# A two-layer decoder step on one core: one unit of output weights, the product's last right sides and its buffers moved in program order

## The chip, the cores and the metric

The kernel runs on one core of a Trainium2 chip. The metric is the device time of one execution in microseconds, lower is better. A launch does one step of the whole trunk: weights and inputs come from HBM, and every output goes back there.

## The reference, cut to what matters

Two layers over a stream of 1,024 prompt tokens, 64 sample tokens and 16 meta tokens (1,104 columns of 1,024 features; the second layer has no meta columns and works on 1,088). The first layer is a Mamba-2 mixer, the second sliding-window attention over shared keys and values; each is followed by an MLP with a squared ReLU:

```python
def sq_relu_mlp(h, norm_w, w_up, w_down):
    return h + jnp.square(jax.nn.relu(rmsnorm(h, norm_w) @ w_up)) @ w_down

# second layer
hp = hp + swa_prompt(q_p, k_p, v_p, k_meta, v_meta, attn_sinks[j]) @ w_o[j]
hp = sq_relu_mlp(hp, mlp_norm_w[layer], w_up[layer], w_down[layer])
```

`w_o` is 1,024 x 1,024, `w_up` 1,024 x 4,096. The change touches the product with `w_o` in the second layer and the product with `w_up` in both.

## The kernel before, in words

**Precision.** Every product of float32 numbers is made of three matmuls: each operand is split into a high part, rounded to a shorter format by a cast on ScalarE, and a low part, the rest, by a subtraction on VectorE (activations) or GpSimd (weights). `mm3` (L199 to L206) issues the three, at L204 (high by high), L205 (high weight by low activation) and L206 (low weight by high activation). So a weight's high part is needed first, its low part two matmuls later.

**Weights.** `wunit` (L156) brings one unit of weights. In the first layer it loads the raw weight into a tile `raw` (2 buffers), casts it on ScalarE (L170) and subtracts on GpSimd (L171). In the second layer most units were split before and lie in HBM as a pair, so two loads by SyncE's queue (L163) bring both parts. The tiles `w` are a ring of 6, which is 3 units.

**Order.** The program is written in one order, and a planner, run when the kernel is built, gives every engine its own fixed order from it by an estimate of when each operand is ready; a place in a buffer is given out in program order, and an operation in a new tile waits for the last reader of what lay there. Each engine, and each DMA queue, then works strictly in its order.

**Second layer, attention's end.** `attention` (L1588 on) works through the heads and chunks of columns, and returns the last four of its output units: chunk 1, the second half of the heads, v = 0 to 3. `out_unit` (L1654) loads its weights and makes two blocks of 128 output rows, 24 matmuls in all, then adds the residual, splits the result and hands it to the stream. Before these four, `second_layer` closes attention's pool `ap`, makes X, a tile of the stream (8 x 1,088 per partition), and `stream.load` (L124, its loads at L128) reads the two finished chunks of the stream back from HBM into X and normalises them there; chunk 1 comes from the four units directly.

**The up product.** The first four of 32 column blocks of `w_up` are computed plainly (`plain_up`, L1015; two at a time in the second layer, three and one in the first). The other 28 go in 14 pairs (`up`, L1117; `up_pair`, L1070) by a Strassen-Winograd scheme on 2 x 2 blocks: seven products of sums instead of eight. Left sides are sums of weight blocks (`up_weights`, L1051): a11, s1 = a21 + a22 (the first sum, L1057), a11 - a21 (L1057), s1 - a11 (L1063), a12, a22, a12 - s1. `raw2` loads the pair's raw weights; every third raw tile lies in the pool `rx`, with the sums `s` (2 buffers) and the results `rx`. `wparts` splits a left side: cast on ScalarE (L1047), subtraction on GpSimd (L1048).

**The right sides.** `sides` (L985) makes the seven right sides from the normalised activations, once for both halves k = 0, 1 of the columns. `step(i, k)` forms one of them and splits it (cast at L1011, subtraction at L1012, here called its split):

- 0: b11; 4: b21; 6: b22, as they are;
- 1: t = b12 - b11; 2: b12 = b22 - b12; 3: t = b22 - t; 5: t = b21 - t (subtractions at L989).

In the first layer the activations lie in `hh`, t is b11's own place, and steps 0, 4 and 6 aren't run: those parts lie in S, split for the plain product already. In the second layer they lie in X, t is one of two temporaries (pool `ts`, on the right side of the memory), and steps 0, 4, 5 and 6 write into S, over the columns that the plain product has read; steps 1 to 3 write tiles `T`. The k = 1 half of step 4 writes columns of chunk 1, the last chunk that the plain product reads. Pools are stacks on a left and a right side. After the steps the second layer closes `ts` and the pool of X, places R0 (the buffer for the down product's right side) where X was, and calls `up`, whose pool `rx` comes on the left, above R0.

**Chain.** The pair's first tile is a11 by step 0 (bank `ma`), the second s1 by step 1 (`md` in the first pair), the third a11 - a21 by step 2 (`mc`), the fourth s1 - a11 by step 3 (`mb`); 24 matmuls each for k = 0 and 1 together. Steps 4, 5 and 6 are used by the fifth to seventh. R0 gets its first blocks by SyncE's queue (L1140) during the pairs, and they are split at L1145 and L1146; R0 is multiplied after the up product.

Of the kernel before, what the change touches and what calls it, by code (L numbers as in the profile page):

```python
# [9 lines left out]
F32R = mybir.dt.float32r  # L10
# [6 lines left out]
P = 128  # L17
# [6 lines left out]
META = SEQ + NB * NS  # L24
NM = 16
T = META + NM
# [115 lines left out]
class Kernel:  # L142
# [842 lines left out]
    def sides(self, X, qw, tiles, temps=None):  # L985


        nc = self.nc
        tt = lambda out, x, y: nc.vector.tensor_tensor(out=out, in0=x, in1=y, op=ALU.subtract)  # L989
        at = lambda j, q: tuple(self.S[:, e, 4 * j:4 * j + 4, q * qw:q * qw + qw] for e in range(2))  # L990
        self.qw = qw
        self.xo = [{0: at(0, q), 4: at(1, q), 5: at(0, p), 6: at(1, p)} for q, p in PAIRS]
        B = [[[X[:, 4 * j:4 * j + 4, q * qw:q * qw + qw] for q in qs] for j in range(2)] for qs in PAIRS]

        def step(i, k):
            (b11, b12), (b21, b22) = B[k]
            t = b11 if temps is None else temps[k]
            src = {0: b11, 1: t, 2: b12, 3: t, 4: b21, 5: t, 6: b22}[i]
            if i == 1:
                tt(t, b12, b11)  # L1000
            elif i == 2:
                tt(b12, b22, b12)
            elif i == 3:
                tt(t, b22, t)
            elif i == 5:
                tt(t, b21, t)
            if i not in self.xo[k]:
                o = tiles()
                self.xo[k][i] = o[:, 0], o[:, 1]
            hi, lo = self.xo[k][i]  # L1010
            nc.scalar.copy(out=hi, in_=src)  # L1011
            nc.vector.tensor_tensor(out=lo, in0=src, in1=hi.bitcast(F32), op=ALU.subtract)  # L1012
        return step

    def plain_up(self, layer, fs, chs, rd, rs=None):  # L1015

# [50 lines left out]
        yield self.wparts(a22, sh)  # L1067
        yield self.wparts(add(a12, s1, ALU.subtract), sh)

    def up_pair(self, layer, f, rd, rt):  # L1070


        nc = self.nc
        qw = self.qw
        n = 2 * qw
        banks = {}
        tt = lambda out, x, y: nc.vector.tensor_tensor(out=out, in0=x, in1=y, op=ALU.add)
        tmp = lambda: self.n3().rearrange("p a b -> p (a b)")[:, :n]
        r = self.rx.tile([P, 4, n], F32, tag="rx", bufs=1, name="rx")

        for i, (wh, wl) in enumerate(self.up_weights(layer, f)):
            b = self.CHAIN[f % 2][i]
            first = b not in banks
            if first:
                banks[b] = self.pq.tile([P, 1024], F32, tag=b, bufs=1, name="m" + b)
            for k in range(2):
                xh, xl = self.xo[k][i]
                self.mm3(banks[b][:, 512 + (k - 1) * qw:512 + k * qw], [(wh[:, q], wl[:, q]) for q in range(4)],
                         [(xh[:, q], xl[:, q]) for q in range(4)], first)
            pv = banks[b][:, 512 - qw:512 + qw]  # L1090
            if i == 0:
                m1 = tmp()
                nc.scalar.copy(out=m1, in_=pv)
            elif i == 1:
                nc.scalar.copy(out=r[:, 3], in_=pv)
            elif i == 2:
                tt(r[:, 3], pv, r[:, 3])
            elif i == 3:
                u = tmp()
                tt(u, pv, m1)  # L1100
                tt(r[:, 3], r[:, 3], u)
            elif i == 4:
                nc.scalar.activation(out=r[:, 0], in_=pv, func=AF.Relu)
            else:
                tt(r[:, 7 - i], pv, u)
            e = {3: 3, 4: 0, 5: 2, 6: 1}.get(i)
            if e is None:
                continue
            if i != 4:
                nc.scalar.activation(out=r[:, e], in_=r[:, e], func=AF.Relu)  # L1110
            nc.scalar.activation(out=r[:, e], in_=r[:, e], func=AF.Square)
        if not 2 <= f < 14:
            nc.sync.dma_start(out=rd[f].rearrange("p f (i n) -> p (f i) n", i=2), in_=r)
            return
        self.side_sums([r[:, e] for e in range(4)], rt[(f - 2) // KB][:, :, :, (f - 2) % KB], m1, u)

    def up(self, layer, rd, rt, R0):  # L1117

        with ExitStack() as cq:
            self.rx = self.pool("rx", ctx=cq)  # L1120
            self.ws = self.rx
            self.rawi = 0
            self.pq = self.pool("pq", space=PSUM, ctx=cq)
            for f in range(2, 16):
                self.up_pair(layer, f, rd, rt)
                if f == 8:
                    self.block_load(rd, 0, R0)
                if f > 11:
                    self.block_parts(f - 12, R0)

    def load_stream(self, big, h_d):

# [518 lines left out]
                half, sp = 0, None  # L1651
        return outs

    def out_unit(self, c, n, prs, v, a, xs, stream):  # L1654

        nc = self.nc
        ws = [self.wunit(self.i["w_o"][pr, v], 4, 256, key=("o", pr, v)) for pr in prs]
        last = prs[-1] == 1
        for m in range(2):
            u, ms = 2 * v + m, slice(m * P, m * P + P)  # L1660
            pt = self.gps()[:, :n]
            self.mm3(pt, [(wh[:, k, ms], wl[:, k, ms]) for wh, wl in ws for k in range(4)],
                     [tuple(e[:, :n] for e in x) for x in a])
            xh, xl = (x[:, u, :n] for x in xs[c])
            h = stream.place(c, u, n) if last else self.n1("hs")[:, :n]
            nc.vector.tensor_tensor(out=h, in0=pt, in1=xl.bitcast(F32), op=ALU.add)
            nc.vector.tensor_tensor(out=h, in0=h, in1=xh.bitcast(F32), op=ALU.add)
            nc.scalar.copy(out=xh, in_=h)
            (nc.vector if c == 1 and last else nc.gpsimd).tensor_tensor(out=xl, in0=h, in1=xh.bitcast(F32),
                                                                        op=ALU.subtract)  # L1670
            if last:
                stream.done(c, u, h)
# [110 lines left out]
    def first_layer(self, cb):  # L1783
# [6 lines left out]
        with ExitStack() as ch:  # L1790
# [20 lines left out]
                self.out_last(hts, done, norm)  # L1811
            with ExitStack() as ct:
                tp = self.pool("T", ctx=ct)
                step = self.sides(big, T // 4, lambda: tp.tile([P, 2, 4, T // 4], F32R, tag="T", bufs=6, name="T"))
                with ExitStack() as ce:
                    self.banks(ce, 8)
                    plain = self.plain_up(0, (0, 1, 2), dict(enumerate(CH)), rd)
                    next(plain)
                    norm(2)
                    for _ in plain:  # L1820
                        pass
                    for _ in self.plain_up(0, (3,), dict(enumerate(CH)), rd):
                        pass
                for i in (1, 2, 3, 5):
                    for k in range(2):
                        step(i, k)
                ch.close()
                R0 = self.pool("R0", ctx=ch, right=True).tile([P, 2, 4, T], F32R, name="R0")
                self.up(0, rd, rt, R0)
# [12 lines left out]
    def second_layer(self, nx, cb):  # L1842
# [6 lines left out]
        with ExitStack() as cx:  # L1849
            cr = ExitStack()  # L1850
            with ExitStack() as c1:
# [11 lines left out]
                tmp = self.pool("att", ctx=cr, right=True)  # L1863
                stream = Stream(self, chs, h_d, self.ncol(3), ps)
                outs = self.attention(nx, ap, tmp, ps, chs, stream)
            stream.load(self.pool("X", ctx=cx).tile([P, KT, META], F32, name="X"))
            for e in outs:
                self.out_unit(*e)
            cr.close()
            tp = self.pool("T", ctx=cr, right=True)  # L1870
            with ExitStack() as ce:
                ts = self.pool("ts", ctx=ce, right=True)
                temps = [ts.tile([P, 4, qw], F32, name="t%d" % k) for k in range(2)]
                step = self.sides(stream.X, qw, lambda: tp.tile([P, 2, 4, qw], F32R, tag="T", bufs=6, name="T"), temps)
                self.more_banks(ce, 5, 0)
                plain = self.plain_up(1, (0, 1), {c: chs[c] for c in (0, 2, 1)}, rd, stream.rs)
                next(plain)
                stream.norm(1)
                for _ in plain:
                    pass  # L1880
                for i in (1, 2, 3):
                    for k in range(2):
                        step(i, k)
                for _ in self.plain_up(1, (2, 3), {c: chs[c] for c in (0, 2, 1)}, rd, stream.rs):
                    pass
                for i in (0, 4, 5, 6):
                    for k in range(2):
                        step(i, k)
            cb.close()
            cx.close()  # L1890
            R0 = self.pool("R0", ctx=cx).tile([P, 2, 4, META], F32R, name="R0")
            self.up(1, rd, rt, R0)
            cr.close()
            big = self.pool("h2", right=True).tile([P, KT, META], F32, name="hh")
            self.load_stream(big, h_d)
# [131 lines left out]
```

## Time and profile before

| what | value |
|---|---|
| time of three runs | 2918.50, 2924.53, 2924.64 us; median 2924.53 |
| the profiled execution | 2923.57 us, its span 2921.9 us |
| TensorE's mean granted clock | 0.986 of full speed |
| busy share of the span | TensorE 96%, VectorE 65%, ScalarE 48%, GpSimd 47% |
| mean DMA rate | 148 GB/s |

The span runs from the first to the last instruction of the profiled execution; the execution's own time is 1.7 us longer. Times in the rows are microseconds from the span's start. In a timeline a row is: start, duration, engine, line, operation, tiles out<-in, size, number of instructions; a row with a number above x1 is several of the same kind one behind the other, and its duration is theirs together. In brackets stands the engine's idle time before it, and what ended it. Engines: PE is TensorE, DVE VectorE, ACT ScalarE, POOL GpSimd, SPq SyncE's DMA queue. "A <- B: x, n, y" in a table of waits reads: A waited x us for B, n times, at the longest y.

### The profile page before, as it was taken

The page shows a single profiled execution, that of the slowest core. Times are in us where ns is not written, and L with a number is a line of the kernel's source. Part 1 is how long each engine was busy: PE and PEld are TensorE (multiplying, and loading weights), DVE is VectorE, ACT ScalarE, POOL GpSimd, SP SyncE. Part 2 cuts the span into 40 slices and gives each one's busy share as a digit, 9 for nine tenths or more (in the row PEclk, how much of TensorE's full clock was granted, in tenths as well). Part 3 has the DMA queues.
Part 4 walks back from the last instruction along what each step waited for, and adds up shares of the span by engine and source line. Part 5 has one row for each costly group of instructions (what it writes and reads, how often), then busy time and mean ns, then how long its engine had stood idle before and what let it go on. Part 6 is the DMA issues. An engine that isn't in the chain of part 4 may idle for free.

```text
span 2921.9 us, 51729 instructions
## 1 busy us (share of the span) xinstructions
PE 2816.2 (96%) x19895; PEld 2711.0 (93%) x19895; DVE 1895.0 (65%) x2995; ACT 1413.9 (48%) x2742; POOL 1386.1 (47%) x1279
## 2 busy tenths in 40 slices
PE   8999999988989999999999999999999999999998
PEld 6999999978889999999999999988889999999998
DVE  6788777765657675455466765666678454356675
ACT  6555555544555264444343325655555444433333
POOL 5566666665546615444266573312112444345562
PEclk9999999999999999999999999999999999999998
DMA  3344544447655224444554422447453444533422
GB/s 137 91 128 124 125 128 123 123 123 258 218 206 171 80 85 149 136 156 139 224 212 171 161 89 94 160 153 261 164 187 133 150 140 150 206 138 124 151 96 73
DMA packets 219470, 433.43 MB, mean 148 GB/s; under 512 B 30728, under 2 KB 128392, under 8 KB 216648
## 3 DMA queue, kind: packets, MB, share of 16 engines
q1 hardware_dynamic: 219224, 430.14, 44.3%
q8 instruction: 156, 2.56, 0.4%
q14 instruction: 90, 0.74, 0.1%
HBM read 302.71 MB, written 128.32 MB: 148 GB/s over the span
## 4 chain that ended last, share of the span: by engine, by line
PE 77%; DVE 10%; ACT 4%; issue 3%; DMA 3%; POOL 3%; SPq 0%; DVEq 0%; ACTq 0%; POOLq 0%
PE g L204 10%; PE g L206 10%; PE g L205 10%; PE mc L204 4%; PE mc L206 3%; PE mc L205 3%; PE ma L204 3%; PE ma L205 3%; PE ma L206 3%; PE md L206 3%; PE md L205 3%; PE md L204 3%; PE mb L206 3%; PE mb L204 3%; PE mb L205 3%
## 5 line engine op out<-in xcount | busy, mean ns | idle before, releaser
L1048 POOL TENSOR_TENSOR w<-s,w 128x384 fp32r<-128x384 f32 (+1 forms) x272 | 370.4, 1368 | 386.9 <-ACT w L1047 354.4
L206 PE MATMUL g<-S,w 128*128 128x384 f32 (+2 forms) x1584 | 531.1, 336 | 3.9 <-POOL w L171 3.3
L204 PE MATMUL g<-S,w 128*128 128x384 f32 (+2 forms) x1584 | 533.4, 337 | 1.3 <-DVE qp L1462 0.6
L205 PE MATMUL g<-S,w 128*128 128x384 f32 (+2 forms) x1584 | 533.6, 337 | 0.0
L1048 POOL TENSOR_TENSOR w<-raw,w 128x384 fp32r<-128x384 f32 (+1 forms) x204 | 264.3, 1301 | 286.2 <-ACT w L1047 255.2
L171 POOL TENSOR_TENSOR w<-raw,w 128x1024 fp32r<-128x1024 f32 x96 | 247.1, 2574 | 253.3 <-ACT w L170 189.3
L206 PEld LDWEIGHTS g<-S,w 128*128 128x128 f32 x1584 | 301.9, 191 | 5.8 <-POOL w L171 3.6
L204 PEld LDWEIGHTS g<-S,w 128*128 128x128 f32 x1584 | 301.3, 190 | 4.7 <-issue 1.5
L205 PEld LDWEIGHTS g<-S,w 128*128 128x128 f32 x1584 | 301.7, 190 | 0.9 <-issue 0.3
L1047 ACT CAST w<-s 128x384 fp32r<-128x384 f32 (+1 forms) x272 | 149.8, 557 | 313.0 <-DVE s L1172 84.7
L204 PE MATMUL ma<-S,w 128*128 128x276 f32 (+1 forms) x808 | 235.2, 291 | 8.0 <-DVE us L1264 6.7
L206 PE MATMUL ma<-S,w 128*128 128x276 f32 (+1 forms) x808 | 234.7, 290 | 0.0
L205 PE MATMUL ma<-S,w 128*128 128x276 f32 (+1 forms) x808 | 234.3, 290 | 0.0
L1047 ACT CAST w<-raw 128x384 fp32r<-128x384 f32 (+1 forms) x204 | 111.8, 555 | 154.6 <-PE mc L206 45.2
L602 DVE SCALAR_TENSOR_TENSOR fm<-xp,cv,fm 128x1024 f32<-128x1024 f32 x96 | 162.8, 1698 | 33.1 <-ACT fm L583 32.5
L204 PEld LDWEIGHTS ma<-S,w 128*128 128x128 f32 x808 | 153.3, 190 | 9.3 <-ACT S L1229 2.7
L205 PE MATMUL g<-R,w 128*128 128x384 f32 (+2 forms) x480 | 158.6, 330 | 0.0
L204 PE MATMUL g<-R,w 128*128 128x384 f32 (+2 forms) x480 | 158.1, 329 | 0.0
L206 PE MATMUL g<-R,w 128*128 128x384 f32 (+2 forms) x480 | 158.1, 329 | 0.0
L205 PEld LDWEIGHTS ma<-S,w 128*128 128x128 f32 x808 | 153.5, 190 | 0.0
L206 PEld LDWEIGHTS ma<-S,w 128*128 128x128 f32 x808 | 153.2, 190 | 0.0
L170 ACT CAST w<-raw 128x1024 fp32r<-128x1024 f32 x96 | 100.5, 1047 | 105.8 <-DMA raw<-in_w_o_dram 19.9
(492 smaller groups left out, 8696.0 us busy)
## 6 DMA issues: line engine op xcount, KB each, us to landing
raw<-in_w_up_dram SPq DMA_DIRECT2D x64, 512.0 KB
raw<-in_w_in_dram SPq DMA_DIRECT2D x48, 512.0 KB
raw<-in_w_downs_dram SPq DMA_DIRECT2D x64, 384.0 KB
w<-ws_o SPq DMA_DIRECT2D x48, 512.0 KB
w<-ws_q SPq DMA_DIRECT2D x40, 512.0 KB
ab<-acs_d SPq DMA_DIRECT2D x64, 256.0 KB
S<-t_d SPq DMA_DIRECT2D x18, 828.0 KB
S<-t_e SPq DMA_DIRECT2D x18, 816.0 KB
```

The lines of the kernel that those rows point to most:

```text
L170: nc.scalar.copy(out=wh, in_=raw)
L171: nc.gpsimd.tensor_tensor(out=wl, in0=raw, in1=wh.bitcast(F32), op=ALU.subtract)
L204: mm(out=out, lhsT=wh, rhs=xh, start=(first and k == 0), stop=False)
L205: mm(out=out, lhsT=wh, rhs=xl, start=False, stop=False)
L206: mm(out=out, lhsT=wl, rhs=xh, start=False, stop=(k == n - 1))
L602: nc.vector.scalar_tensor_tensor(out=acc[:, :SEQ], in0=xp[:, k:k + SEQ], scalar=cv[:, j, k:k + 1], in1=acc[:, :SEQ], op0=ALU.mult, op1=ALU ...
L1047: nc.scalar.copy(out=t[:, 0], in_=src)
L1048: nc.gpsimd.tensor_tensor(out=t[:, 1], in0=src, in1=t[:, 0].bitcast(F32), op=ALU.subtract)
```

## The change

Three edits, which leave every sum and product what it was.

1. `out_unit` gets its weights handed in, or asks for them by `out_weights`. In `second_layer` the first of the last four units asks for its weights ahead of `stream.load`.
2. In `sides` step 5 no longer writes t. A new function `diff(k)` writes b21 = b21 - t in place, and step 5 splits b21. The first layer calls `diff(k)` just ahead of step 5; the second calls both behind step 4, with steps 5 and 6 left for later.
3. In the second layer `up` gets a function `sides(i)`, called in the first pair behind the result of tile i: step 5 at i = 0, step 6 at i = 1, and at i = 6 X's pool is closed and R0 placed. For that call the pool `rx` is opened on the right side.

```diff
@@ sides
             t = b11 if temps is None else temps[k]
-            src = {0: b11, 1: t, 2: b12, 3: t, 4: b21, 5: t, 6: b22}[i]
+            src = {0: b11, 1: t, 2: b12, 3: t, 4: b21, 5: b21, 6: b22}[i]
...
-            elif i == 5:
-                tt(t, b21, t)
...
-        return step
+
+        def diff(k):
+            b21 = B[k][1][0]
+            tt(b21, b21, B[k][0][0] if temps is None else temps[k])
+        return step, diff
@@ up_pair
-    def up_pair(self, layer, f, rd, rt):
+    def up_pair(self, layer, f, rd, rt, more=None):
...
-        banks = {}
+        banks, R0 = {}, None
...
                 tt(r[:, 7 - i], pv, u)
+            if more is not None:
+                R0 = more(i)
@@ up
-    def up(self, layer, rd, rt, R0):
+    def up(self, layer, rd, rt, R0, sides=None):
         with ExitStack() as cq:
-            self.rx = self.pool("rx", ctx=cq)
+            self.rx = self.pool("rx", ctx=cq, right=sides is not None)
...
             for f in range(2, 16):
-                self.up_pair(layer, f, rd, rt)
+                R0 = self.up_pair(layer, f, rd, rt, sides if f == 2 else None) or R0
@@ out_unit
-    def out_unit(self, c, n, prs, v, a, xs, stream):
-
-        nc = self.nc
-        ws = [self.wunit(self.i["w_o"][pr, v], 4, 256, key=("o", pr, v)) for pr in prs]
+    def out_weights(self, prs, v):
+        return [self.wunit(self.i["w_o"][pr, v], 4, 256, key=("o", pr, v)) for pr in prs]
+
+    def out_unit(self, c, n, prs, v, a, xs, stream, ws=None):
+
+        nc = self.nc
+        ws = ws or self.out_weights(prs, v)
@@ first_layer
                 for i in (1, 2, 3, 5):
                     for k in range(2):
+                        if i == 5:
+                            diff(k)
                         step(i, k)
@@ second_layer
+            ws = self.out_weights(*outs[0][2:4])
             stream.load(self.pool("X", ctx=cx).tile([P, KT, META], F32, name="X"))
             for e in outs:
-                self.out_unit(*e)
+                self.out_unit(*e, ws)
+                ws = None
...
-                for i in (0, 4, 5, 6):
+                for i in (0, 4):
                     for k in range(2):
                         step(i, k)
+                for k in range(2):
+                    diff(k)
             cb.close()
-            cx.close()
-            R0 = self.pool("R0", ctx=cx).tile([P, 2, 4, META], F32R, name="R0")
-            self.up(1, rd, rt, R0)
+
+            def sides(i):
+
+                if i < 2:
+                    for k in range(2):
+                        step(5 + i, k)
+                if i == 6:
+                    cx.close()
+                    return self.pool("R0", ctx=cx).tile([P, 2, 4, META], F32R, name="R0")
+            R0 = self.up(1, rd, rt, None, sides)
             cr.close()
```

## Rows read from the trace of the kernel before

**Rows 1.** The page's head.
```profile
span 2921.9 us, 51729 instructions
```

**Rows 2.** TensorE's waits, 2100 to 2400 us: total, times, longest.
```profile
PE g L204 <- DMA w<-ws_o: 3.4, 1, 3.4
PE md L204 <- ACT w L1047: 3.2, 1, 3.2
...
PE md L206 <- POOL w L1048: 0.2, 1, 0.2
```

**Rows 3.** TensorE's waits, 900 to 1200 us, same columns.
```profile
PE g L206 <- POOL w L171: 3.3, 1, 3.3
```

**Rows 4.** SyncE's queue, 2060 to 2182 us: start, duration.
```profile
2117.29 37.28 SPq L163 DMA_DIRECT2D w<-ws_o  x14
2173.75 1.59 SPq L128 DMA_DIRECT2D X<-h_e  x2
2175.45 2.22 SPq L163 DMA_DIRECT2D w<-ws_o  x2
```

**Rows 5.** SyncE's queue, 2150 to 2280 us: its waits, as in rows 2.
```profile
SPq L128 <- PE yb L1529: 19.1, 1, 19.1
...
SPq L163 <- PE g L206: 4.7, 2, 4.3
```

**Rows 6.** Stretches: length, busy time per engine, TensorE's granted clock, DMA share, GB/s.
```profile
2247.50:2251.00 3.50, 3.41 (x15) 3.41 (x16) 1.74 (x1) 1.06 (x2) 1.27 (x2) 0.52 1.01 379
873.80:878.00 4.20, 4.15 (x18) 4.15 (x19) 4.17 (x3) 3.57 (x5) 3.16 (x3) 0.50 0.20 78
```

**Rows 7.** TensorE's waits, 860 to 890 us.
```profile
PE md L204 <- ACT w L1047: 6.2, 1, 6.2
PE md L206 <- POOL w L1048: 1.8, 1, 1.8
```

**Rows 8.** VectorE ahead of the second layer's first pair.
```profile
2239.56 1.29 DVE L1012 TENSOR_TENSOR S<-X,S 128x1088 fp32r<-128x1088 f32 x1 [1.63 <-ACT S L1011]
...
2241.24 1.28 DVE L1012 TENSOR_TENSOR S<-t,S 128x1088 fp32r<-128x1088 f32 x1
2242.43 2.49 DVE L1012 TENSOR_TENSOR S<-X,S 128x1088 fp32r<-128x1088 f32 x2
2244.84 1.29 DVE L1057 TENSOR_TENSOR s<-raw 128x512 f32<-128x512 f32 x2
```

**Rows 9.** ScalarE in the same stretch.
```profile
2240.44 2.09 ACT L1011 CAST S<-X 128x1088 fp32r<-128x1088 f32 x2
...
2245.56 1.22 ACT L1047 CAST w<-s 128x512 fp32r<-128x512 f32 x2 [1.83 <-DVE s L1057]
```

**Rows 10.** GpSimd in the same stretch.
```profile
2218.30 4.28 POOL L1048 TENSOR_TENSOR w<-raw,w 128x512 fp32r<-128x512 f32 x1 [52.98 <-ACT w L1047]
2246.25 2.51 POOL L1048 TENSOR_TENSOR w<-s,w 128x512 fp32r<-128x512 f32 x2 [23.68 <-DMA raw<-in_w_up_dram]
```

**Rows 11.** VectorE ahead of the first layer's first pair.
```profile
1090.93 1.30 DVE L989 TENSOR_TENSOR hh<-hh 128x1104 f32<-128x1104 f32 x1
...
1094.59 2.52 DVE L1012 TENSOR_TENSOR T<-hh,T 128x1104 fp32r<-128x1104 f32 x2
1103.40 1.29 DVE L1057 TENSOR_TENSOR s<-raw 128x512 f32<-128x512 f32 x2 [6.30 <-DMA raw<-in_w_up_dram]
...
1105.83 4.72 DVE L989 TENSOR_TENSOR hh<-hh 128x1104 f32<-128x1104 f32 x2
```

**Rows 12.** GpSimd in the same stretch.
```profile
1090.75 8.55 POOL L171 TENSOR_TENSOR w<-raw,w 128x1024 fp32r<-128x1024 f32 x1 [39.81 <-ACT w L170]
...
1104.83 4.56 POOL L1048 TENSOR_TENSOR w<-s,w 128x512 fp32r<-128x512 f32 x2 [4.28 <-ACT w L1047]
```

**Rows 13.** All operations of line 171: duration in ns, minimum, median, maximum.
```profile
L171 POOL TENSOR_TENSOR w<-raw,w x96: 2343/2398/8552, 10.5 to 2866.4; 128x1024 fp32r<-128x1024 f32 x96
```

**Rows 14.** TensorE at the first layer's second tile.
```profile
1115.80 0.29 PE L204 MATMUL md<-T,w 128*128 128x276 f32 x1
```

More of the change, by code (lines that the diff above doesn't have):

```diff
@@ L1113, in up_pair @@
             nc.sync.dma_start(out=rd[f].rearrange("p f (i n) -> p (f i) n", i=2), in_=r)
-            return
+            return R0
         self.side_sums([r[:, e] for e in range(4)], rt[(f - 2) // KB][:, :, :, (f - 2) % KB], m1, u)
-    def up(self, layer, rd, rt, R0):
+        return R0
+    def up(self, layer, rd, rt, R0, sides=None):
         with ExitStack() as cq:
-            self.rx = self.pool("rx", ctx=cq)
+            self.rx = self.pool("rx", ctx=cq, right=sides is not None)
             self.ws = self.rx
@@ L1129, in up @@
                     self.block_parts(f - 12, R0)
+        return R0
     def load_stream(self, big, h_d):
@@ L1813, in first_layer @@
                 tp = self.pool("T", ctx=ct)
-                step = self.sides(big, T // 4, lambda: tp.tile([P, 2, 4, T // 4], F32R, tag="T", bufs=6, name="T"))
+                step, diff = self.sides(big, T // 4, lambda: tp.tile([P, 2, 4, T // 4], F32R, tag="T", bufs=6, name="T"))
                 with ExitStack() as ce:
@@ L1873, in second_layer @@
                 temps = [ts.tile([P, 4, qw], F32, name="t%d" % k) for k in range(2)]
-                step = self.sides(stream.X, qw, lambda: tp.tile([P, 2, 4, qw], F32R, tag="T", bufs=6, name="T"), temps)
+                step, diff = self.sides(stream.X, qw, lambda: tp.tile([P, 2, 4, qw], F32R, tag="T", bufs=6, name="T"), temps)
                 self.more_banks(ce, 5, 0)
```

## The prediction, made before any run of the changed kernel

> **What bounds the kernel now.** I read four views, in this order. First the page's head: the span is 2921.9 us [rows 1], the execution 2923.57 us, 0.96 under the median of the three runs, 2924.53. TensorE is busy for 96% of it, so the only time a change of order can move is TensorE's own idle time and the slow stretches behind it. 0.2% of the median, about what a measurement of this kernel can tell from no change, is 5.85 us: faster means under 2918.7, slower over 2930.4.
>
> Second, TensorE's waits around the edited lines. In the second layer there are two long ones and a short one [rows 2]: 3.4 us in the output projection for weights by DMA (call it stall A), and in the first pair of the up product 3.2 us for ScalarE's cast of the second left side, with 0.2 us behind it for GpSimd's part of the same tile (stall B). The first layer has one of 3.3 us, late in its plain up columns, for GpSimd's low part of a weight (stall C) [rows 3].
>
> Third, SyncE's queue, which issues the loads of stall A [rows 4, 5]. Fourth, the timelines of VectorE, ScalarE and GpSimd ahead of stalls B and C [rows 8 to 12].
>
> **What a stall costs beyond its wait.** [...] A longer pair of waits elsewhere, 6.2 and 1.8 us with only two matmuls between [rows 7], is followed by 4.2 us at 0.50: 2.1 us lost, some 2.4 with its edges [rows 6]. [...]
>
> **Part 1, the weights requested ahead of the reload.** The edit moves one unit's two DMA requests (the first of the last four units) ahead of the two X loads in program order. The queue already has them there: 14 requests, seven units, go out before the X loads, and only the last unit's two stand behind them, at 2175.45 [rows 4]. Seven units are the four of the other half and the first three of the last four. X waited 19.1 us for attention's last reader; the request behind it waited for a matmul too, the shorter of two waits that sum to 4.7 with a longest of 4.3, so 0.4 us [rows 5]. With six weight tiles, three units, the fourth can't be asked for before the first's matmuls end, and the edit gives no further tile. So the pair of requests that TensorE waits for isn't the pair that moves: 0 us. If the planner does put the last pair first, its 3.4 us of waiting and some 1.6 at the slow clock go: 5.0 us. X would then arrive later by 0.5 MB of loads; its normalisation lies behind another unit of matmuls.
>
> **Part 2, the difference in place.** Step 5 no longer writes the temporary but b21. Two subtractions per layer remain, of the same size, about 1.25 us each in a run [rows 11]; nothing is added, but what they wait for changes.
>
> In the first layer the old form overwrites the block that step 3's split still reads, so it stands behind step 3: the trace has both at 1105.83, after the pair's first sums [rows 11]. The new form needs only step 3's subtraction, and b21, whose split was done with the plain columns. Both differences are then ready while VectorE still splits steps 2 and 3, and they come ahead of the sums, which wait for a raw tile until 1103.40. VectorE's run, which ends at 1097.1 [rows 11], becomes 2 x 1.22 = 2.4 us longer.
>
> That run covers GpSimd's low part of the weight that stall C waits for. The operation took 8.55 us [rows 12], where the 96 of its line have a median of 2.40 and a minimum of 2.34 [rows 13]. It began at 1090.75, from 1090.93 VectorE went through five two-input operations without a gap until 1097.1 [rows 11], and GpSimd was done at 1099.3, 2.2 us later: it got next to nothing done before VectorE went idle. So each operation put on the end of the run delays stall C's end by its length. I take 2.4 us of wait and 0.4 of clock, **+2.8**; the ends are 0 (they land elsewhere) and three operations, with step 3's second split, 3.7 + 0.5 = 4.2.
>
> [...]
>
> What follows stall C has cover: the pair's second left side is needed at 1115.80 [rows 14], and GpSimd is done with it at 1109.4 [rows 12]; a raw load moved by 2.4 us fits into 6.4.
>
> **Part 3, the second layer's last right sides.** Steps 5 and 6 move behind the first tile of the first pair in program order; X is given back only at that pair's end, and R0, whose first loads go out in this stretch, is placed then. R0 is first multiplied after the up product; 13 pairs cover it: 0. The rx pool (the sums s, the third raw, the results) moves from the left, where X's and other tiles must be done first, to the right, where the two temporaries lay. This is meant to let VectorE make the sums early: before stall B it idled 1.63 us ahead of the operation at 2239.56 [rows 8], and the sums came last, at 2244.84.
>
> But the temporaries' last reader is now the second difference, diff(1). It overwrites a block which step 4's split still reads, and that split writes S columns of the chunk which the plain matmuls read until just before stall B. In the old order VectorE goes 2239.56 (step 0), 2241.24 (step 5), 2242.43 (steps 4 and 6), sums [rows 8]. In the new one diff(1) can go only behind step 4's split; step 6's split, whose cast is done by 2242.5 [rows 9], is ready first. I get diff(1) from 2244.84 to 2246.06 and the sum behind it, 0.65, to 2246.7. ScalarE is by then given step 5's cast of the second half, ready at 2246.1: 2 casts take 2.09, so 1.05 [rows 9], to 2247.2; then the sum's cast, 0.6 (two take 1.22), to 2247.8. In the old order that cast was done by 2246.2. So +1.6. Then GpSimd's part: alone it took 1.25 (two in 2.51) and TensorE waited only 0.2 for it [rows 2, 10], but now VectorE has step 5's second split to do from about 2247.3 to 2248.6. Another operation of this line that met such a run took 4.28 us [rows 10]. GpSimd is done at about 2249.85 where it was 2247.5: **+2.3** of wait, 0.4 of clock, **+2.7**.
>
> Bounds: +0.4 if diff(1) goes straight behind step 4, the sums take its old place and GpSimd is undisturbed; at the top another split runs ahead of GpSimd, +1.25 more, 4.1 with clock; at the bottom the sums are made in the gap as meant, and 3.2, 0.2 and 1.7 all go: -5.1. Between these I take the row order, in which what is ready first goes first. Late next, were stall B gone, would be the fourth tile's weights, which are made from the same sums and move with them.
>
> **The sum.** 0 + 2.8 + 2.7 = 5.5 on the profiled execution's 2923.57: **2929.1 us**, 4.5 over the median, still within 0.2%. Its own range is 2926 to 2931.
>
> **The rivals.**
> *The sums come on time.* If the planner gives the sums their place before diff(1), as a place of the rx pool that overlaps only the first temporary would allow, stall B goes: -5.1 + 2.8 = 2921.3, or 2918.5 if the first layer doesn't pay. For it: VectorE has idle time there. Against it: the rows show the sums waiting behind every split though nothing they compute needs one, so the whole place must be free. 0.18.
>
> *First come, first served.* GpSimd gets in at the next boundary whatever VectorE has queued; stall C doesn't grow: 2923.57 + 2.7 = 2926.3, less if GpSimd's 0.7 at stall B goes too. Against it the 8.55 us [rows 12]. 0.17. [...]
>
> *GpSimd is shut out for whole runs (slower).* The mechanism of stall C decides in both places: in the first layer three operations join the run (+4.2), in the pair two splits are ready when ScalarE's cast is done (+4.1): 8.3, **2931.9 us**. It decides from the point where VectorE has two or more such operations ready when GpSimd starts; with the pair alone and 2.8 for the first layer it is 6.9, 2930.5, just over the bound. For it 8.55 and 4.28 us [rows 10, 12]; against it that GpSimd's part in the old pair met an idle VectorE, which waited for it. 0.15.
>
> *The last weights do come early.* -5.0: with the other two terms 2924.1, with the sums on time too 2916.3. Against it the slots [rows 5]. 0.08.
>
> The forecast keeps 0.42. That part 1 doesn't do what it says is in all cases but the last.
>
> **How the numbers follow.** Faster needs the sums on time and the first layer free, or both gains: 0.17 with what I don't see. Slower is most of the shut-out and the top fifth of the forecast: 0.22. The rest, 0.61, lies within 0.2%. The range goes from under both gains with the first layer's cost (2916.3) to over the shut-out (2931.9): 2915.5 to 2932.5. Outside are both gains without that cost (2913.5) and a re-planned order elsewhere.
>
> **What would show it.** Stall A: a DMA wait of about 3.4 us before the last unit stands as before; if it is gone, part 1 worked. Stall C: the two in-place subtractions ahead of the sums, the GpSimd operation some 11 us long, TensorE's wait 5.7 us; 3.3 means first come, first served. Stall B: diff(1) just ahead of the sums, step 5's cast ahead of theirs, TensorE's first wait 4.8 us and the one for GpSimd near 0.9; sums made before 2242.7 mean that the change works as meant, and that I read their place wrongly. A total under 2915.5 or over 2932.5 would mean that a cost or gain lies where I haven't looked.

## The result, and the profile after

The changed kernel takes 2929.75 us, the median of 11 runs (2927.00 to 2933.32); the kernel before, on the same chip, 2923.93 (2918.50 to 2924.64). The medians lie 5.8 us apart. The ratio of the runs is 1.0022 with a 95% interval of 1.0013 to 1.0030: some 6.4 us slower, 3.8 to 8.8. The forecast was 2929.1. The profiled execution's span grew by 6.1 us, TensorE's busy time by 0.3:

```profile
span 2928.0 us, 51730 instructions
...
PE 2816.5 (96%) x19895; PEld 2711.5 (93%) x19895; DVE 1895.9 (65%) x2995; ACT 1416.6 (48%) x2742; POOL 1385.2 (47%) x1279
```

TensorE's waits, first layer and second, in the stretches of [rows 3] and [rows 2]:

```profile
PE g L206 <- POOL w L171: 5.7, 1, 5.7
```

```profile
PE md L204 <- ACT w L1050: 4.3, 1, 4.3
PE g L204 <- DVE X L1676: 3.3, 1, 3.3
PE md L206 <- POOL w L1051: 0.6, 1, 0.6
```

Stall C went from 3.3 to 5.7 us. Stall B went from 3.2 and 0.2 to 4.3 and 0.6. Stall A is as long as before, but the trace now names VectorE's add instead of the weights' DMA. Lengths between fixed matmuls of TensorE's timeline say what each is worth, clock included. From attention's last matmul to the last output matmul it is 18.35 us before and 18.42 after (A). From the last plain chunk's first matmul of 384 columns to the pair's first it is 17.18 and 19.96 (C: +2.8). From the pair's first to the fourth tile's first it is 14.92 and 17.44 (B: +2.5). The stretch between A and B and that from B to the down product differ by 0.02 us at most. So 5.4 of the 6.1 us lie in the two stalls; 0.7 is left over in stretches that the edits don't touch, where two runs of one order differ by more (first experiment).

**Stall A.** SyncE's queue, as in [rows 4]: the same 14 requests ahead of X, the same two behind it.

```profile
2119.32 37.26 SPq L163 DMA_DIRECT2D w<-ws_o  x14
2175.75 1.46 SPq L128 DMA_DIRECT2D X<-h_e  x2
2177.31 2.35 SPq L163 DMA_DIRECT2D w<-ws_o  x2
```

**Stall C.** VectorE and GpSimd ahead of it, as in [rows 11, 12]:

```profile
1092.76 1.30 DVE L990 TENSOR_TENSOR hh<-hh 128x1104 f32<-128x1104 f32 x1
1093.98 1.30 DVE L1011 TENSOR_TENSOR T<-hh,T 128x1104 fp32r<-128x1104 f32 x1
1095.20 1.30 DVE L990 TENSOR_TENSOR hh<-hh 128x1104 f32<-128x1104 f32 x1
1102.78 1.29 DVE L1060 TENSOR_TENSOR s<-raw 128x512 f32<-128x512 f32 x2 [6.29 <-DMA raw<-in_w_up_dram]
```

```profile
1087.70 10.99 POOL L171 TENSOR_TENSOR w<-raw,w 128x1024 fp32r<-128x1024 f32 x1 [38.72 <-ACT w L170]
```

The rows of L990 at 1092.76 and 1095.20 are the two in-place differences, which stood behind the sums before. From GpSimd's start at 1087.70 VectorE now does seven two-input operations without a gap, where it did five, and ends at 1096.5 (1095.20 + 1.30); GpSimd ends at 1098.7, 2.2 us later, as before. The operation is 10.99 - 8.55 = 2.44 us longer, which is two operations of 1.22.

**Stall B.** VectorE, ScalarE and GpSimd ahead of it, as in [rows 8 to 10], and the clock behind it, as in [rows 6]:

```profile
2241.13 1.29 DVE L1011 TENSOR_TENSOR S<-X,S 128x1088 fp32r<-128x1088 f32 x1 [2.69 <-ACT S L1010]
...
2242.81 3.69 DVE L1011 TENSOR_TENSOR S<-X,S 128x1088 fp32r<-128x1088 f32 x3
2246.41 1.28 DVE L990 TENSOR_TENSOR X<-X,t 128x1088 f32<-128x1088 f32 x1
2247.62 1.28 DVE L1060 TENSOR_TENSOR s<-raw 128x512 f32<-128x512 f32 x2
2248.86 1.29 DVE L1011 TENSOR_TENSOR S<-X,S 128x1088 fp32r<-128x1088 f32 x1
```

```profile
2247.73 1.10 ACT L1010 CAST S<-X 128x1088 fp32r<-128x1088 f32 x1 [1.94 <-DVE X L990]
2248.74 1.14 ACT L1050 CAST w<-s 128x512 fp32r<-128x512 f32 x2
```

```profile
2249.43 3.14 POOL L1051 TENSOR_TENSOR w<-s,w 128x512 fp32r<-128x512 f32 x2 [24.78 <-ACT w L1050]
```

```profile
2251.40:2255.50 4.10, 4.10 (x18) 4.10 (x19) 2.41 (x2) 2.35 (x5) 2.82 (x3) 0.50 0.92 362
```

The order is the one worked out: the splits of steps 5, 4 and 6 (2242.81), the second half's difference (2246.41), then the two sums (2247.62). ScalarE casts step 5's block first (2247.73), then the sums (2248.74); VectorE's last split (2248.86) runs into GpSimd's part, whose first half ends near 2251.3, where TensorE goes on.

### The profile page after: what moved, and what is told of

It is laid out like the page before. It is cut to its first block, busy times and chain, and to the rows that moved or that the text cites. A ratio compares the mean times of both kernels' runs of the same rounds, so it can differ in the third digit from the quotient of the medians.

```text
span 2928.0 us, 51730 instructions
## 1 busy us (share of the span) xinstructions
PE 2816.5 (96%) x19895; PEld 2711.5 (93%) x19895; DVE 1895.9 (65%) x2995; ACT 1416.6 (48%) x2742; POOL 1385.2 (47%) x1279
## 4 chain that ended last, share of the span: by engine, by line
PE 74%; DVE 9%; issue 6%; DMA 4%; POOL 4%; ACT 3%; SPq 0%; DVEq 0%; POOLq 0%; ACTq 0%
PE g L204 10%; PE g L206 9%; PE g L205 9%; PE mc L204 3%; PE mc L206 3%; PE mc L205 3%; PE ma L204 3%; PE ma L206 3%; PE ma L205 3%; PE mb L204 2%; PE mb L206 2%; PE mb L205 2%; PE md L206 2%; PE md L205 2%; PE md L204 2%
```

## The experiments

Each was timed on the same chip as the kernel before; ratios are to that. In this table A and B are the lengths named above, "later" is from the fourth tile to the down product, C the wait for the low part of the weight, all from TensorE's timeline and waits in the profiled execution. Between A and B lie 48.3 us, but 48.1, 48.7, 49.0 and 50.0 in the four kernels that ask for the last weights early, in the order of the table. In the pieces of code "..." stands for lines left out.

| kernel | ratio, 95% interval | A us | B us | later us | C us |
|---|---|---|---|---|---|
| before | 1 | 18.35 | 14.92 | 287.1 | 3.3 |
| changed | 1.0022 (1.0013 to 1.0030) | 18.42 | 17.44 | 287.1 | 5.7 |
| weights alone | 0.9999 (0.9990 to 1.0008) | 18.69 | 14.90 | 287.3 | 3.2 |
| first layer alone | 1.0007 (0.9998 to 1.0015) | 18.23 | 14.86 | 287.1 | 5.7 |
| second layer alone | 1.0012 (1.0003 to 1.0021) | 18.42 | 17.42 | 287.1 | 3.3 |
| longer run | 1.0020 (1.0011 to 1.0028) | 18.78 | 17.56 | 287.1 | 5.7 |
| changed, own sums | 1.0008 (0.9999 to 1.0017) | 18.43 | 9.90 | 289.7 | 5.7 |
| changed, low part on VectorE | 0.9990 (0.9982 to 0.9999) | 19.22 | 17.76 | 287.1 | 0 |
| before, last weights early | 0.9993 (0.9984 to 1.0002) | 17.21 | 16.83 | 288.8 | 3.2 |
| before, weights and normalisation | 0.9997 (0.9989 to 1.0006) | 13.16 | 17.02 | 288.9 | 3.3 |
| before, own sums | 1.0000 (0.9992 to 1.0009) | 18.76 | 14.66 | 287.1 | 3.2 |
| before, sums and low part | 0.9990 (0.9982 to 0.9999) | 18.53 | 15.76 | 287.1 | 0 |
| before, all three | 0.9986 (0.9978 to 0.9995) | 12.94 | 17.69 | 289.0 | 0 |
| changed, all three | 0.9993 (0.9984 to 1.0002) | 12.94 | 16.06 | 294.1 | 0 |

### Edit 1 alone

```diff
+            ws = self.out_weights(*outs[0][2:4])
             stream.load(...)
             for e in outs:
-                self.out_unit(*e)
+                self.out_unit(*e, ws)
+                ws = None
```

> The kernel before with edit 1 alone: the first of the last four output units asks for its weights ahead of the reload. My theory: the queue already had that pair of requests ahead of X, and the pair that TensorE waits for is the last unit's, so nothing moves: stall A stays 3.3 to 3.4 us, the same order in SyncE's queue, time within 1.5 us of the kernel before. Rival (the edit does what it says): stall A goes, 3.4 us of waiting and some 1.6 at the slow clock, 5.0 us faster.

Measured 2924.58 against 2924.41 us, with a DMA wait of 3.5 us in A. The order on every engine is the one before. So edit 1 does nothing. The run's profiled span is 1.7 us shorter than that of the kernel before, which is how far two executions of one order lie apart.

### The first layer's part alone, and the second's

```diff
-            src = {..., 5: t, 6: b22}[i]
+            src = {..., 5: b21 if temps is None else t, 6: b22}[i]
...
-            elif i == 5:
-                tt(t, b21, t)
+            elif i == 5 and temps is None:
+                tt(b21, b21, t)
+            elif i == 5:
+                tt(t, b21, t)
```

> The kernel before with the in-place difference in the first layer alone; the second layer is as before. My theory: VectorE's run ahead of the pair's first sums becomes two operations (2.4 us) longer, GpSimd's low part of the last plain weight takes 11.0 instead of 8.55 us, stall C is 5.7 instead of 3.3 us, 2.8 us slower in all, clock included; stalls A and B as in the kernel before. Rival (GpSimd gets in at the next boundary): 8.5 us and 3.3 us, no change.

Measured 2927.34 us, 2.9 over the median before; the interval goes from 0.6 us under to 4.4 over it, so the time alone doesn't show a loss. The trace does: the wait is 5.7 us, and GpSimd's operation is the long one:

```profile
1088.64 10.99 POOL L171 TENSOR_TENSOR w<-raw,w 128x1024 fp32r<-128x1024 f32 x1 [38.73 <-ACT w L170]
```

The other half, the changed kernel with the first layer's old form:

```diff
...
+            if temps is None:
+                tt(B[k][0][0], b21, B[k][0][0])
+            else:
+                tt(b21, b21, temps[k])
```

> The changed kernel, with the first layer's fifth difference written as in the kernel before. My theory: stall C is back at 3.3 us and its GpSimd operation at 8.5; stall B stays at 4.3 and 0.6 us; against the changed kernel 2.8 us faster, against the kernel before 2.6 to 3 us slower. Rival (the two layers' parts aren't independent, or the loss of the changed kernel lies elsewhere): as slow as the changed kernel, 5 to 6 us over the kernel before.

Measured 2927.43 us, 3.0 over. TensorE's waits in it:

```profile
PE md L204 <- ACT w L1053: 4.3, 1, 4.3
...
PE g L206 <- POOL w L171: 3.3, 1, 3.3
...
PE md L206 <- POOL w L1054: 0.6, 1, 0.6
```

Each part has its own stall and leaves the other's alone, and the two losses, 2.9 and 3.0 us, add up to the whole.

### A longer run for GpSimd to wait out

```diff
             tt(b21, b21, ...)
+            if temps is None and k == 0:
+                nc.vector.tensor_tensor(out=b21, in0=b21, in1=B[k][0][0], op=ALU.add)
+                tt(b21, b21, B[k][0][0])
```

> The changed kernel with two more VectorE operations in the first layer, behind the first half's difference: b21 + t and minus t again, both with two inputs in SBUF, which leave b21 as it was up to rounding. My theory (GpSimd is kept out while VectorE goes from one such operation to the next): the GpSimd operation takes 10.99 + 2.44 = 13.4 us, stall C 5.7 + 2.4 = 8.1 us, time 2.8 us over the changed kernel, 8.5 over the kernel before. Rival (GpSimd waits for one operation, whichever is first goes first): 11.0 and 5.7 us, no change against the changed kernel.

Measured 2930.25 us and 5.7 us of wait, the rival's numbers, but not for its reason. VectorE in it:

```profile
1093.27 1.30 DVE L990 TENSOR_TENSOR hh<-hh 128x1104 f32<-128x1104 f32 x1
1100.83 1.30 DVE L1063 TENSOR_TENSOR s<-raw 128x512 f32<-128x512 f32 x2 [6.25 <-DMA raw<-in_w_up_dram]
1102.04 1.30 DVE L1011 TENSOR_TENSOR T<-hh,T 128x1104 fp32r<-128x1104 f32 x1
1103.26 2.40 DVE L1017 TENSOR_TENSOR hh<-hh 128x1104 f32<-128x1104 f32 x1
```

The planner put the added pair (the first of it at 1103.26, L1017) behind the sums, so the run that GpSimd's low part meets ends with the same operation as in the changed kernel. At stall C nothing was added, and the run doesn't tell the theories apart there; what does is five operations against seven, 8.55 us against 10.99. But the added operation at 1103.26, behind the pair's first sums, took 2.40 us instead of 1.30, as long as each of the two differences that stand there beside GpSimd's parts in the kernel before (4.72 for both [rows 11, 12]): that fits GpSimd getting in at the next boundary, as the rival has it.

### The low part on VectorE

```diff
-        nc.gpsimd.tensor_tensor(out=wl, in0=raw, in1=wh.bitcast(F32), op=ALU.subtract)
+        (low or nc.gpsimd).tensor_tensor(out=wl, in0=raw, in1=wh.bitcast(F32), op=ALU.subtract)
```

with `low=nc.vector` for the first layer's column block 3 alone.

> The changed kernel with the low part of the first layer's last plain weight made on VectorE instead of GpSimd. My theory (that operation needs 2.4 us on GpSimd and is only kept out by VectorE): made inside VectorE's own run it takes 1.2 us, stall C (5.7 us and 1.7 of clock) goes, 7 us faster than the changed kernel, about 1.5 us faster than the kernel before; GpSimd's next operation, for the pair's first tile, then meets the run instead, with cover till the pair. Rival (the cast or the weight's load is late, not GpSimd): a wait of the same size for another engine, no gain.

Measured 2923.23 us against 2924.63 before: the ratio fell from 1.0022 to 0.9990, about 9 us where 7 were expected, which the intervals don't tell apart. VectorE and GpSimd in it:

```profile
1094.06 1.22 DVE L171 TENSOR_TENSOR w<-raw,w 128x1024 fp32r<-128x1024 f32 x1
```

```profile
1094.70 10.25 POOL L1052 TENSOR_TENSOR w<-raw,w 128x512 fp32r<-128x512 f32 x1 [43.07 <-ACT w L1051]
```

The operation that took GpSimd 10.99 us takes VectorE 1.22. Stall C is gone, and GpSimd's next one, for the pair's first tile (1.27 us elsewhere), now waits out the run in its place: 10.25 us, covered, as nobody needs it yet.

### A place of their own for the sums

```diff
+                self.sw = self.pool("sw", ctx=cr, right=True)
                 ts = self.pool("ts", ctx=ce, right=True)
...
-            self.ws = self.rx
+            self.ws = self.sw or self.rx
```

> The changed kernel with a pool of their own, beside the tiles T, for the pair's sums and the third raw tile, opened ahead of the steps; it overlaps neither X nor the temporaries. My theory (the sums wait only for the place, which is given back by the second half's difference): VectorE makes the first two sums while it waits elsewhere, long before that difference; stall B (4.3 and 0.6 us, and 1.9 of clock behind it) goes, 6.8 us faster than the changed kernel, about 1 us faster than the kernel before. Rival (the sums come late because of their turn behind the splits, or their raw tiles): stall B as in the changed kernel, no gain.

Measured 2927.68 us; the ratio fell from 1.0022 to 1.0008, some 4 us of the 6.8. VectorE, and TensorE later:

```profile
2198.69 1.28 DVE L1060 TENSOR_TENSOR s<-raw 128x512 f32<-128x512 f32 x2
...
2248.38 6.53 DVE L1011 TENSOR_TENSOR S<-X,S 128x1088 fp32r<-128x1088 f32 x3
2254.84 1.28 DVE L990 TENSOR_TENSOR X<-X,t 128x1088 f32<-128x1088 f32 x1
...
2257.28 1.29 DVE L1011 TENSOR_TENSOR S<-X,S 128x1088 fp32r<-128x1088 f32 x1
```

```profile
2282.33 0.39 PE L204 MATMUL ma<-S,w 128*128 128x272 f32 x1 [2.23 <-ACT n L1096]
```

The sums are made at 2198.69, some 50 us earlier, and stall B is gone: 17.44 to 9.90 us. So the place held them. But three splits now take 6.53 us (2248.38) where they took 3.69, 2.18 each, near the 2.35 that one took beside a part of GpSimd's in the next run, and the second half's difference (2254.84) and the last split (2257.28) stand before the first pair's results, so VectorE comes late to those: TensorE waits 2.2 us at 2282.33 for ScalarE's copy into a tile that VectorE reads, and 2.65 us of the gain are given back.

The same place in the kernel before:

> The kernel before with a pool of their own for the pair's sums and third raw tile, and nothing of the change. My theory (stall B is a wait for the sums' place in both kernels): the first two sums are made some 40 us early and stall B (3.2 and 0.2 us, 1.7 of clock) goes, 5.1 us. In the changed kernel 2.7 us of such a gain were given back in the first pairs' results, where VectorE had fallen behind; here no difference stands behind step 4, so I expect 3 to 5 us less than the kernel before. Rival (the earlier sums only push VectorE's splits back, which TensorE then waits for): under 1.5 us.

Measured 2922.28 against 2922.28 us: the rival. TensorE, VectorE and GpSimd in it:

```profile
2241.23 0.59 PE L205 MATMUL ma<-S,w 128*128 128x272 f32 x1 [4.01 <-DVE S L1012]
```

```profile
2235.93 1.77 DVE L1057 TENSOR_TENSOR s<-raw,s 128x512 f32<-128x512 f32 x1 [0.74 <-POOL w L1048]
2237.62 1.28 DVE L1012 TENSOR_TENSOR S<-t,S 128x1088 fp32r<-128x1088 f32 x1
2238.82 2.35 DVE L1012 TENSOR_TENSOR S<-X,S 128x1088 fp32r<-128x1088 f32 x1
```

```profile
2238.33 1.69 POOL L1048 TENSOR_TENSOR w<-raw,w 128x512 fp32r<-128x512 f32 x1 [1.18 <-ACT w L1047]
```

Stall B has gone to the first tile, where TensorE waits 4.0 us for step 0's split (2238.82). That split took 2.35 instead of 1.28 us, as GpSimd was at a weight of the same pair at 2238.33, and a later sum (2235.93) stood ahead. The early sums bring their casts and GpSimd's parts forward too, into the stretch in which VectorE's splits are the longest chain.

### The weights that stall A waits for

```diff
+    def out_weights(self, prs, v):
+        ws = [self.raw([P, 4, 256]) for _ in range(2)]
...
+            ws = self.out_weights(*outs[-1][2:4])
             stream.load(...)
...
+                self.out_unit(*e, ws=ws if e is outs[-1] else None)
```

> The kernel before with what edit 1 meant: the weights of the last of the four units come into the two raw tiles, free at that time, and are asked for long before the reload of X. What I now think of stall A: two things end it within 0.1 us, the weights and the PSUM bank, which VectorE's add gives back only behind eight normalisations of X (4.3 us). Then the wait is 3.3 us as before, but for VectorE, and the time is within 1.5 us of the kernel before. Rival (the weights alone hold the unit): stall A goes, 5 us faster.

Measured 2924.30 against 2924.63 us. The wait of 3.4 us for these weights is gone, and none for VectorE takes its place: the planner put plain matmuls in between, and TensorE waits there instead, for the plain product's weights:

```profile
2183.77 0.61 PE L204 MATMUL g<-S,w 128*128 128x320 f32 x1 [2.37 <-DMA w<-ws_up]
```

A is 1.1 us shorter, B 1.9 and the pairs behind it 1.7 longer: what A gives is more than given back in the profiled execution. Whether VectorE's add alone would have held the unit stays open. With the normalisation held back as well:

```diff
-        for c in list(self.rs):
-            self.norm(c)
+        self.held = list(self.rs)
...
+            with self.tc.issue_after(self.add):
+                for c in stream.held:
+                    stream.norm(c)
```

> As the run with the last unit's weights in the raw tiles, and VectorE's normalisation of X queued behind the last unit's add. My theory (both ended stall A): the wait of 3.4 us and the slow clock behind it (1.6) go; the plain product's first weights are then needed 4 us earlier, in a stretch where DMA moves 390 GB/s without a gap, which may give back up to 1 us: 4 to 5 us faster than the kernel before. Rival (something else frees the unit, or the plain product's weights only become the next wait): under 1.5 us.

Measured 2923.81 against 2924.63 us: the rival in its sum. Stall A is gone (18.35 to 13.16 us, the 5 that were estimated), but TensorE then waits longer at the pair:

```profile
2245.46 0.59 PE L203 MATMUL md<-T,w 128*128 128x272 f32 x1 [4.87 <-ACT w L1046]
```

B is 2.1 us longer, the pairs behind 1.8, and the ratio doesn't tell the rest from nothing.

### All repairs together

Three more kernels are made of the edits shown above and nothing else.

> The kernel before with the sums' own pool and the low part of the first layer's last plain weight on VectorE, nothing of the change. My theory (stalls B and C lie in different layers and add up): stall C's 3.3 us and 1.6 of clock go as well, 8 to 10 us less than the kernel before. Rival (one of them comes back as another wait): 4 to 5 us less.

> As the run before this one, and the last output unit's weights in the raw tiles ahead of the reload, with VectorE's normalisation of X behind the last add. By themselves these two gave nothing, since stall B grew by what stall A gave. My theory (VectorE's chain up to the sums was what the two stalls shared, and the sums are off it now): stall A's 3.4 us and 1.6 of clock now show, 11 to 15 us less than the kernel before. Rival (the splits themselves, or the saturated DMA, hold TensorE 3 to 5 us later): no less than with the sums and the low part alone.

> The same three repairs in the changed kernel: own pool for the sums, the low part on VectorE, the last unit's weights in the raw tiles with the normalisation behind. My theory: all three stalls go, 15 to 19 us less than the changed kernel; the second half's difference behind step 4 still puts VectorE 1.3 us back before the first pair's results, so it ends 0 to 3 us over the same repairs in the kernel before. Rival (with the sums free the moved steps are an advantage): 1 us or more under them.

Measured 2918.50, 2917.50 and 2921.03 against 2922.28 us. The first two beat both kernels, 0.10% and 0.14% under the one before, though the changed kernel with the low part on VectorE alone had reached 0.10% too. The third takes back 8.5 of the 15 to 19 us expected (1.0022 to 0.9993). All three expectations were too high, about twofold or more: what is left of the gain is the first layer's, since in the second TensorE waits for VectorE wherever it gets early. In the kernel with all three repairs it waits 6.2 us at the first tile for step 0's split:

```profile
2239.09 0.59 PE L204 MATMUL ma<-S,w 128*128 128x272 f32 x1 [6.18 <-DVE S L1011]
```

In the changed kernel with all three it waits 4.0 us at the sixth tile, for the bank that VectorE's first result gives back:

```profile
2255.75 0.59 PE L203 MATMUL mc<-S,w 128*128 128x272 f32 x1 [4.00 <-DVE rx L1080]
```

## Why the prediction was right

**Part 1, 0 us:** as forecast, and shown by edit 1 alone. The reading of the queue held: the pair of requests that moves was already ahead. What the prediction lacked is that the weights weren't alone. In the trace of the changed kernel the same wait of 3.3 us has another name:

```profile
2187.64 0.41 PE L204 MATMUL g<-ah,w 128*128 128x384 f32 x1 [3.34 <-DVE X L1676]
```

```profile
2182.80 4.32 DVE L138 SCALAR_TENSOR_TENSOR X<-X,nv,acc 128x384 f32<-128x384 f32 x8
2187.03 0.55 DVE L1676 TENSOR_TENSOR X<-g,S 128x384 f32<-128x384 f32 x1
```

VectorE's add, which gives a PSUM bank back, stood behind eight normalisations of X. In the kernel before, the same add had ended at 2185.58, 0.2 us before the weights let TensorE go on:

```profile
2185.03 0.55 DVE L1666 TENSOR_TENSOR X<-g,S 128x384 f32<-128x384 f32 x1
2185.75 0.42 PE L204 MATMUL g<-ah,w 128*128 128x384 f32 x1 [3.44 <-DMA w<-ws_o]
```

**Part 2, +2.8 us:** wait 5.7 us and operation "some 11 us" forecast, 5.66 and 10.99 measured; the stage +2.8. The first layer alone and the low part on VectorE show it from both sides. The rival of first come, first served would have left 3.3 us of wait; at stall C it fell. GpSimd's operation had begun before all seven of VectorE's (1087.70) and got done only behind the last. For others the rival holds, in the prediction's own rows: from 1104.83 two of GpSimd's parts took 4.56 us, and VectorE's two differences beside them 4.72 instead of 2.5 [rows 11, 12], so there GpSimd got in between. The prediction read one operation rightly and passed over the other; what sets the two apart is taken up in the last section.

**Part 3, +2.7 us:** +2.5 measured, by the order that was worked out, operation by operation. Its two terms were mis-sized against each other. The waits grew by 1.5 us (3.4 to 4.9), not 2.3, as VectorE began the last splits 0.5 us earlier in relation to TensorE's last plain matmul, and the four matmuls between the two waits ran 0.2 us longer (the clock granted from 2249.90 to 2250.80 was 0.50), so that less was left of the second wait. The clock cost 1.0 more, not 0.4: 4.1 us and more at a granted 0.50 [rows 6 had 3.5 at 0.52]. That the two errors leave only 0.2 us is luck. The 0.4 us of clock in parts 2 and 3, and the 0.5 at the top of part 2, were my estimate, and no run shows them: in the changed kernel C's stretch grew by 0.4 us beyond its wait (3.26 to 5.66 us) and B's by 1.0. The 1.6 and 1.7 us of clock in the terms for stalls A and B agree with the kernel before: 4.50 us at a granted 0.62 from 2185.70 (A), 3.50 at 0.52 [rows 6] (B).

**The rivals.** "The sums come on time" needed a place that overlaps only the first temporary; the sums came behind the second half's difference, so that reading of the place held, and with a place of their own they did come on time. "Shut out for whole runs" failed on its condition: only one split was ready when ScalarE's cast was done. "The last weights do come early" fell with part 1.

**The chances.** 5.5 us over the profiled execution was called within 0.2%; the medians lie 5.82 apart and the ratio says 0.22%. The result stands on the bound between "same" and "slower"; the sum was right, and a chance of 0.22 for slower was low for a forecast so near it.

## What to carry to other kernels

An edit in a shared helper is paid wherever the helper is called: half of this loss lies in the layer that the change wasn't about. When a wait has one name in the trace, look at what ended second: removing stall A or B alone gave nothing in the kernel before, since VectorE's chain of splits ended just behind both. And a low part on GpSimd that begins beside a run of two-input VectorE operations can cost the run's length and not its own, here 10.99 us where its line's median is 2.40 [rows 13]: look at the operation's own row, since the same kernel has others that cost one turn (4.56 us for two, where one takes 1.27 alone).

## What the runs showed of the hardware

Where GpSimd's subtraction met operations of VectorE with both inputs in SBUF, the traces show two outcomes.

**Kept out for the run.** Here VectorE went on with its next operation at each boundary: GpSimd's 2.4 us operation took 8.55 and 10.99 us in runs of five and seven, its 1.27 us one 10.25 us. In the rows below it got in where VectorE's next operation read PSUM. GpSimd and VectorE in the changed kernel:

```profile
2220.36 4.28 POOL L1051 TENSOR_TENSOR w<-raw,w 128x512 fp32r<-128x512 f32 x1 [53.04 <-ACT w L1050]
```

```profile
2222.20 1.28 DVE L1011 TENSOR_TENSOR T<-X,T 128x1088 fp32r<-128x1088 f32 x1
2223.41 0.55 DVE L1032 SCALAR_TENSOR_TENSOR n<-g,acc 128x384 f32<-128x384 f32 x1
2223.87 1.92 DVE L990 TENSOR_TENSOR t<-X,t 128x1088 f32<-128x1088 f32 x1
```

The operation at 2223.41 reads a PSUM bank (g); GpSimd's work, waiting since 2220.36, ends 1.2 us after it starts, at 2224.64, and then VectorE's next two-input operation pays: 1.92 us instead of 1.28.

**Taking turns.** In the kernel before, GpSimd's two parts from 1104.83 and VectorE's two differences from 1105.83 [rows 11, 12] went one after the other: 4.56 us for the two on GpSimd, where one takes 1.27 alone, and 4.72 us for the two on VectorE, where one takes 1.30. The second difference was ready, as the split that it waits for had ended at 1105.9, and still GpSimd got in ahead of it. These differences are of the same form as those in stall C's run, so the form of VectorE's operations doesn't tell the two outcomes apart.

What goes with the outcome in the traces of the two kernels is how long GpSimd had been idle. Of its weight subtractions that began 0.1 us or more before the end of a VectorE TENSOR_TENSOR with both inputs in SBUF, with another such right behind, six were kept out past the next boundary, three in each kernel, and each came after 29 to 53 us of idle time (39.81 and 38.72 at stall C, 53.04 above); those that got in at the next boundary came after 5.1 us at most. No run changed this idle time by itself, so whether it is the cause stays open.

I hadn't expected how often VectorE pays in turn: with the sums early in the kernel before, step 0's split took 2.35 us instead of 1.28 beside a part of GpSimd's, and TensorE's wait of 4.0 us for that split stood where the gain should have been.
